# Hybrid Hyena/attention/pooling backbone: the norms' subtraction, the pooling's ends and a few priorities put elsewhere

## The chip, the cores and the metric

The kernel runs on one core of a Trainium2 chip. The metric is the device time of one execution in microseconds (us), the median of three runs. A core has TensorE (PE, matmuls; PEld is its weight load), VectorE (DVE), ScalarE (ACT), GpSimd (POOL) and SyncE (SP, which here issues most DMAs). Each engine runs its own instructions in order; semaphores order them between engines.

## The reference

Two layers over 256 latent and 256 context tokens, 1024 wide, all float32. Each layer modulates its input with a scale and a shift, makes one large input projection, and from its columns three mixers: a Hyena long convolution (a 3-tap short convolution, then a product in the frequency domain), grouped-query attention with normed queries and keys and rotary positions, and centred pooling over windows of 2, 4, 8 and 16 tokens. Each mixer has a projection and a gate; their sum goes through an output projection, a residual and a norm. A SwiGLU FFN with a residual and a norm follows. What is touched here, cut short:

```python
def layer_norm(x, g, b):
    mu = jnp.mean(xf, axis=-1, keepdims=True)
    var = jnp.mean(jnp.square(xf - mu), axis=-1, keepdims=True)
    return (xf - mu) * lax.rsqrt(var + EPS) * g + b

# pool_mixer, per group of 256 channels with window w
    lo, hi = jnp.clip(t - w // 2, 0, L), jnp.clip(t + w - w // 2, 0, L)
    mean = (csg[:, hi] - csg[:, lo]) / (hi - lo)       # fewer tokens at both ends
    outs.append(mean - uf)

# hyena_mixer: s = b + sum over 3 taps of up[:, j:j+L] * w[j]; then v, x0, x1 = split(s)

# trunk_layer
    xl = layer_norm(DN_ALPHA * xl + g1_l * stream_mixer(...), ln1_g, ln1_b)
    xl = layer_norm(DN_ALPHA * xl + g2_l * swiglu(xl * (1 + sc2_l) + sh2_l), ln2_g, ln2_b)
```

In the second layer only the latent stream is carried through (256 tokens); the context gives keys and values alone.

## The kernel before

Features lie on the 128 partitions, tokens along the free axis: a stream of activations is eight tiles of 128 features by 512 tokens in layer 0 (latent, then context) and by 256 in layer 1. A float32 product is made of three matmuls on parts: a value is split into a rounded part (hi) and the rest (lo), and hi x hi, hi x lo and lo x hi are added up in PSUM (`mm3`, L165). Weights come as 336 blocks of 128 x 1024 in the order of use (`wfetch`, L203): a DMA, ACT writes hi (L162), VectorE, or for every sixth or third block GpSimd, writes lo by a subtraction (L159). Three blocks of each are buffered. Dense products have three PSUM buffers (`mm`), other products five (`aux`).

The code is a trace of instructions. A planner at build time turns it into a fixed list per engine: whatever is ready and comes first in the trace goes first, and `high_priority(n)` counts an instruction as traced n places earlier. Side chains are Python generators in a list `bg`; each dense block calls `pump` (L130), which moves every generator in `bg` one yield further. `drain` (L150) runs all of them to their end.

A layer runs: Hyena's 24 blocks, where each of the three parts per channel block goes through `short_conv` (L535: one ACT operation, two VectorE taps, L541 and L543, which read PSUM and free it); pooling's eight blocks (`pool_in`, L574: GpSimd clears the padding, ACT copies, VectorE adds shifted copies (L593), GpSimd multiplies the first and last eight tokens (L598), VectorE finishes (L600)); keys and values (`kv`, L656, starts the generator `keys`, L689); a drain; merge of Hyena with its gate; queries; merge of pooling; attention; merge of attention; output projection; norm; FFN; norm.

A norm has two parts. While the eight tiles come out of TensorE, `ln_tile_` (L833) adds the residual (L836), ACT squares (L842), and VectorE adds up the values and squares (L846, L847). Then `ln_finish_` (L867): TensorE sums over partitions and broadcasts (`lnbc`, L852, L874); ACT squares the mean (L876), VectorE makes the variance (L877) and its root by eight steps (`newton`, L286); ACT copies the mean (L879). For each pair of tiles VectorE subtracts the mean (L884) and scales (L885), and the outputs are written, as hi and lo or as they are. In layer 0 both norms run once for each stream. In layer 1 the first norm has work beside it: TensorE takes the unnormed values through five FFN blocks, which `from_raw` (L926) corrects afterwards. The last norm is followed only by the output's DMAs.

The keys' generator, in full order of its pieces:

```python
    def keys(self, kf, sqs, kh):
        ...            # sums of squares (PE), root on 8 columns (DVE)
        yield
        ...            # krb: root spread to all partitions (PE), kf scaled (DVE), swap by DMA (POOL)
        yield
        self.rotate(kf[:, :, 0:SEQ], sw, NKV)
        self.split(kh[0], kh[1], kf)
```

`kv` calls `self.start(self.keys(...))`, which runs it to the first yield, and then, for each of two pairs of value tiles, the value matmuls, a split and `self.pump()`.

## Time and profile before

| | |
|---|---|
| three runs, median (us) | 1705.91 (1705.83 to 1708.21) |
| profiled execution, own time (us) | 1707.7 |
| its span, first to last instruction (us) | 1705.9 |
| mean granted TensorE clock, share of full | 0.989 |
| busy: TensorE, VectorE, ACT, GpSimd (us) | 1652.4, 1222.7, 708.6, 221.5 |

Busy time counts an instruction from its start to its end, and an instruction that is held up after its start is busy for that time too. A wait in the profile has the engine that waited, the line of the waiting instruction and that of the one that released it. Matmuls overlap and their ends are modelled. A granted clock of 1.00 is 2.4 GHz, one of 0.50 is 1.2 GHz; a mean between them is a share of the time at each.

### The profile page before, as it was taken

What the parts mean: (1) busy time and instruction counts of PE and PEld (TensorE: products, weight loads), DVE (VectorE), ACT (ScalarE), POOL (GpSimd) and SP (SyncE); (2) the same over time, 40 slices, a digit from 0 to 9 for tenths busy, and PEclk for the clock granted to TensorE, in tenths of its full rate; (3) what the DMA queues carried; (4) which work ended last, traced back from release to release, by engine and by line L of the source; (5) the groups of instructions that cost most, each with busy time, mean ns of one, the idle gap of its engine ahead of it and who ended that gap; (6) DMA issues with size and microseconds to landing.
All of it is one profiled execution on the core that took longest, in us unless ns stands there. A gap on an engine that the chain in (4) does not pass through costs nothing.

```text
span 1705.9 us, 25592 instructions
## 1 busy us (share of the span) xinstructions
PE 1652.4 (97%) x9926; PEld 1445.9 (85%) x9926; DVE 1222.7 (72%) x2124; ACT 708.6 (42%) x1130; POOL 221.5 (13%) x232
## 2 busy tenths in 40 slices
PE   7999999999999999999999999998899999989996
PEld 1888888788888888988888888898799999989996
DVE  4788878755677775879876577498866786796655
ACT  2534332533454432542232223274435564564442
POOL 1133542000200000000000012124510210000000
PEclk9999999999999999999999999999999999999998
DMA  8422222453422343236666654154336535645552
GB/s 315 158 87 87 74 80 76 148 161 126 136 79 93 122 156 125 92 88 197 190 200 191 211 190 149 62 165 132 100 120 191 166 100 162 195 139 185 185 185 88
DMA packets 68897, 243.34 MB, mean 143 GB/s; under 512 B 8166, under 2 KB 8744, under 8 KB 68520
## 3 DMA queue, kind: packets, MB, share of 16 engines
q1 hardware_dynamic: 67192, 236.78, 43.5%
q0 software_dynamic: 1168, 4.72, 0.9%
q8 instruction: 78, 1.28, 0.3%
q14 instruction: 43, 0.35, 0.1%
q10 hardware_dynamic: 416, 0.21, 0.1%
HBM read 238.01 MB, written 1.05 MB: 140 GB/s over the span
## 4 chain that ended last, share of the span: by engine, by line
PE 82%; DVE 12%; ACT 3%; issue 2%; POOL 1%; DMA 1%; ACTq 0%; DVEq 0%; POOLq 0%
PE f L171 6%; PE f L169 6%; PE f L170 6%; PE b L169 4%; PE g L169 4%; PE g L171 4%; PE g L170 4%; PE b L171 4%; PE b L170 4%; PE w L169 4%; PE w L170 4%; PE w L171 4%; DVE wlo L159 2%; PE ux L169 2%; PE ux L171 2%
## 5 line engine op out<-in xcount | busy, mean ns | idle before, releaser
L162 ACT ACTIVATE whi<-raw 128x1024 fp32r<-128x1024 f32 x322 | 340.7, 1059 | 700.4 <-PE f L170 153.5
L159 DVE TENSOR_TENSOR wlo<-raw,whi 128x1024 fp32r<-128x1024 f32 x311 | 399.9, 1287 | 202.2 <-ACT whi L162 199.6
L190 DVE SCALAR_TENSOR_TENSOR junk<-ada,silu 128x1024 bf16<-128x1024 f32 x128 | 158.9, 1243 | 55.6 <-DMA ada<-adat 55.0
L169 PE MATMUL f<-h2h,whi 128*128 128x512 f32 (+1 forms) x320 | 125.1, 391 | 0.1
L171 PE MATMUL f<-h2h,wlo 128*128 128x512 f32 (+1 forms) x320 | 124.6, 389 | 0.0
L170 PE MATMUL f<-h2l,whi 128*128 128x512 f32 (+1 forms) x320 | 124.6, 389 | 0.0
L169 PE MATMUL f<-h,whi 128*128 128x256 f32 x312 | 88.4, 283 | 1.9 <-DVE fraw L931 1.9
L169 PE MATMUL w<-a,whi 128*128 128x256 f32 (+1 forms) x284 | 90.2, 317 | 0.0
L170 PE MATMUL w<-a,whi 128*128 128x256 f32 (+1 forms) x284 | 89.3, 315 | 0.0
L171 PE MATMUL w<-a,wlo 128*128 128x256 f32 (+1 forms) x284 | 89.3, 314 | 0.0
L171 PE MATMUL f<-h,wlo 128*128 128x256 f32 x312 | 88.5, 283 | 0.6 <-DVE wlo L159 0.6
L170 PE MATMUL f<-h,whi 128*128 128x256 f32 x312 | 87.5, 280 | 0.0
L169 PE MATMUL g<-hh,whi 128*128 128x512 f32 x192 | 75.6, 394 | 0.0
L171 PE MATMUL g<-hh,wlo 128*128 128x512 f32 x192 | 75.4, 393 | 0.0
L170 PE MATMUL g<-hl,whi 128*128 128x512 f32 x192 | 75.3, 392 | 0.0
L169 PEld LDWEIGHTS f<-h2h,whi 128*128 128x128 f32 x320 | 60.0, 188 | 14.0 <-DVE sg L974 0.9
L171 PEld LDWEIGHTS f<-h2h,wlo 128*128 128x128 f32 x320 | 60.1, 188 | 13.6
L170 PEld LDWEIGHTS f<-h2l,whi 128*128 128x128 f32 x320 | 60.2, 188 | 13.1
L169 PEld LDWEIGHTS f<-h,whi 128*128 128x128 f32 x312 | 58.6, 188 | 2.3 <-issue 2.3
L170 PEld LDWEIGHTS f<-h,whi 128*128 128x128 f32 x312 | 59.3, 190 | 0.0
L171 PEld LDWEIGHTS f<-h,wlo 128*128 128x128 f32 x312 | 58.4, 187 | 0.8 <-DVE wlo L159 0.8
L170 PEld LDWEIGHTS w<-a,whi 128*128 128x128 f32 x284 | 53.5, 188 | 3.9 <-issue 0.2
(474 smaller groups left out, 4799.6 us busy)
## 6 DMA issues: line engine op xcount, KB each, us to landing
raw<-wst SPq DMA_DIRECT2D x336, 512.0 KB, 3.6
ada<-adat SPq DMA_DIRECT2D x80, 512.0 KB, 4.1
adar<-ada SPq DMA_DIRECT2D x16, 512.0 KB, 10.2
qsw<-q POOLq DMA_DIRECT2D x16, 128.0 KB, 5.0
x<-x_t POOLq DMA_DIRECT2D x1, 2048.0 KB, 9.7
x<-x_t SPq DMA_DIRECT2D x1, 1024.0 KB, 10.5
x<-x_t SPq DMA_DIRECT2D x2, 512.0 KB, 10.2
silu<-c_row SPq DMA_DIRECT2D x2, 512.0 KB, 8.4
```

The costliest lines, as they stand in the source:

```text
L159: (eng or self.nc.vector).tensor_tensor(out=lo, in0=src, in1=hi.bitcast(F32), op=ALU.subtract)
L162: self.nc.scalar.activation(hi, src, AF.Copy)
L169: t.matmul(out, lhsT=ah, rhs=bh, start=start, stop=False)
L170: t.matmul(out, lhsT=ah, rhs=bl, start=False, stop=False)
L171: t.matmul(out, lhsT=al, rhs=bh, start=False, stop=stop)
L190: nc.vector.scalar_tensor_tensor(out=junk, in0=raw, scalar=1.0, in1=self.silu[:, s], op0=ALU.mult, op1=ALU.mult, accum_out=mod[:, s, m : m ...
```

## The change

The subtraction of the mean (L884) becomes a function `center`. With `beside`, which is set for every norm but the second stream of layer 0's second norm, GpSimd runs all of it, issued behind ACT's copy of the mean and ahead of the root; that copy now stands ahead of the variance. Without it, VectorE subtracts as before, one pair at a time. In layer 1's first norm the additions of values and squares move to GpSimd too. The finish of the first norms has priority 100 instead of none. In layer 1 `short_conv` has priority 100. In pooling, the two memsets become one and the two products at the ends become one, both strided and on VectorE. `drain` takes a generator to leave alone, and `layer` gives it the keys' at the first drain.

```diff
--- before.py
+++ after.py
@@ -147,12 +147,13 @@
         self.bg.append(g)
         self.step(g)
 
-    def drain(self):
-        while self.bg or self.feed:
-            if not self.bg:
+    def drain(self, keep=None):
+        while self.feed or any(g is not keep for g in self.bg):
+            if all(g is keep for g in self.bg):
                 self.start(self.feed.popleft())
             for g in list(self.bg):
-                self.step(g)
+                if g is not keep:
+                    self.step(g)
 
 
     def lo_of(self, lo, src, hi, eng=None):
@@ -532,7 +533,13 @@
             hi, lo = hy[2 * qd + ci]
             self.split(hi[:, t0 : t0 + SEQ], lo[:, t0 : t0 + SEQ], y[:, ci])
 
-    def short_conv(self, l, u, ch, out, ns):
+    def short_conv(self, l, *a):
+        if l == 0:
+            return self.short_conv_(l, *a)
+        with self.tc.high_priority(100):
+            self.short_conv_(l, *a)
+
+    def short_conv_(self, l, u, ch, out, ns):
 
         nc = self.nc
         v = lambda t: t.rearrange("p (s t) -> p s t", s=ns)
@@ -581,8 +588,8 @@
             w = WINDOWS[g]
             u_ps = self.dense(h, T, "up")
             u = self.t4(shape=[P, ns, W], name="pu")
-            nc.gpsimd.memset(u[:, :, 0:PAD], 0.0)
-            nc.gpsimd.memset(u[:, :, PAD + SEQ :], 0.0)
+            eights = lambda t: t.rearrange("p s (k e) -> p s k e", e=8)
+            nc.vector.memset(eights(u)[:, :, 0 :: W // 8 - 1], 0.0)
             nc.scalar.activation(u[:, :, PAD : PAD + SEQ], u_ps.rearrange("p (s t) -> p s t", s=ns), AF.Copy)
 
             cur, step, lo, hi = u, 1, 0, W
@@ -594,9 +601,9 @@
                                         in1=cur[:, :, nlo + b : nhi + b], op=ALU.add)
                 cur, lo, hi = nx, nlo, nhi
                 step *= 2
-            for e, ec in ((PAD, 0), (PAD + SEQ - 8, 8)):
-                nc.gpsimd.tensor_tensor(out=cur[:, :, e : e + 8], in0=cur[:, :, e : e + 8],
-                                        in1=self.edge[:, g : g + 1, ec : ec + 8].to_broadcast([P, ns, 8]), op=ALU.mult)
+            ends = eights(cur[:, :, PAD : PAD + SEQ])[:, :, 0 :: SEQ // 8 - 1]
+            nc.vector.tensor_tensor(out=ends, in0=ends, in1=self.edge[:, g : g + 1].rearrange("p o (a e) -> p o a e", e=8).to_broadcast([P, ns, 2, 8]),
+                                    op=ALU.mult)
             nc.vector.scalar_tensor_tensor(out=po[:, c].rearrange("p (s t) -> p s t", s=ns), in0=cur[:, :, PAD : PAD + SEQ],
                                            scalar=1.0 / w, in1=u[:, :, PAD : PAD + SEQ], op0=ALU.mult, op1=ALU.subtract)
 
@@ -669,7 +676,8 @@
             nc.scalar.activation(kf[:, hh], o, AF.Copy, scale=self.v(l, V_KG))
             sqs.append(sq)
             self.pump()
-        self.start(self.keys(kf, sqs, kh))
+        self.kgen = self.keys(kf, sqs, kh)
+        self.start(self.kgen)
         wa, wb = self.wblock(1), self.wblock(0)
         for tp in range(2):
             o = self.mm([P, 2, 256], name="v")
@@ -816,9 +824,9 @@
                 nc.vector.scalar_tensor_tensor(out=x, in0=x, scalar=scale, in1=cb, op0=ALU.mult, op1=ALU.subtract)
             yield
 
-    def ln_start(self, y, s, g, pt, pf):
+    def ln_start(self, y, s, g, pt, pf, beside=True, sums=None):
         ts = slice(s * SEQ, (s + 1) * SEQ)
-        st = dict(y=y[:, :, ts], g=g[:, s], s=s, pt=pt, pf=pf)
+        st = dict(y=y[:, :, ts], g=g[:, s], s=s, pt=pt, pf=pf, beside=beside, sums=sums or self.nc.vector)
         st["acc"] = self.t2b(shape=[P, 2, SEQ], name="lnacc")
         return st
 
@@ -843,8 +851,8 @@
         if m == KT - 1:
             st["sq"] = sq
             return
-        nc.vector.tensor_tensor(out=acc[:, 0], in0=y[:, 0] if m == 1 else acc[:, 0], in1=d, op=ALU.add)
-        nc.vector.tensor_tensor(out=acc[:, 1], in0=acc[:, 1], in1=sq, op=ALU.add)
+        st["sums"].tensor_tensor(out=acc[:, 0], in0=y[:, 0] if m == 1 else acc[:, 0], in1=d, op=ALU.add)
+        st["sums"].tensor_tensor(out=acc[:, 1], in0=acc[:, 1], in1=sq, op=ALU.add)
 
     def ln_sums(self, st):
 
@@ -874,14 +882,24 @@
             nc.tensor.matmul(bc[:, i], lhsT=self.ones, rhs=src, start=False, stop=i == 1)
         rm = st["rm"] = self.t2b(shape=[P, 2, SEQ], name="lnrm")
         nc.scalar.activation(t, bc[:, 0], AF.Square)
+        nc.scalar.activation(rm[:, 1], bc[:, 0], AF.Copy)
+        steps = [((0, 1), (1, 1)), ((2, 2),), ((4, 2),), ((6, 2),)]
+
+        def center(e, i):
+            for m, n in steps[i // 2]:
+                e.tensor_tensor(out=y[:, m : m + n], in0=y[:, m : m + n], in1=rm[:, 1:2].to_broadcast([P, n, SEQ]), op=ALU.subtract)
+
+        if st["beside"]:
+            for i in range(0, KT, 2):
+                center(nc.gpsimd, i)
         nc.vector.scalar_tensor_tensor(out=a, in0=bc[:, 1], scalar=EPS, in1=t, op0=ALU.add, op1=ALU.subtract)
         self.newton(rm[:, 0], a, t)
-        nc.scalar.activation(rm[:, 1], bc[:, 0], AF.Copy)
         yield
         for i in range(0, KT, 2):
-            for m, n in ((i, 1), (i + 1, 1)) if i == 0 else ((i, 2),):
+            if not st["beside"]:
+                center(nc.vector, i)
+            for m, n in steps[i // 2]:
                 yn = y[:, m : m + n]
-                nc.vector.tensor_tensor(out=yn, in0=yn, in1=rm[:, 1:2].to_broadcast([P, n, SEQ]), op=ALU.subtract)
                 nc.vector.scalar_tensor_tensor(out=yn, in0=yn, scalar=1.0 / RS, in1=rm[:, 0:1].to_broadcast([P, n, SEQ]), op0=ALU.mult, op1=ALU.mult)
             for kind, dst, a, b, *at in outs:
                 td = slice(at[0], at[0] + SEQ) if at else ts
@@ -1027,7 +1045,7 @@
         self.pool_in(l, h, T, po)
         self.lo_pool = 0
         kh, vh = self.kv(l, [(h, 0, 512)] if hc is None else [(h, 0, SEQ), (hc, SEQ, SEQ)])
-        self.drain()
+        self.drain(self.kgen)
         if not last:
             self.bg.append(self.filter_hidden(l + 1))
         mg = self.big(F32, [P, KT, T], name="mg")
@@ -1057,7 +1075,7 @@
         al = self.scaled(self.v(l, V_LN1G, 8), self.v(l, V_LN1B, 8))
         fo = [self.fold(self.v(l, V_LN1G, 8), self.v(l, V_LN1B, 8), mod[4][:, s], mod[3][:, s]) for s in range(ns)]
         raw = self.raw_pair(*fo[0]) if ns == 1 else None
-        lns = [self.ln_start(y, s, mod[2], (20, 50)[l], 0) for s in range(ns)]
+        lns = [self.ln_start(y, s, mod[2], (20, 50)[l], 100, sums=(None, nc.gpsimd)[l]) for s in range(ns)]
         if raw:
             lns[0]["raw"] = raw, fo[0][0]
         for m in range(KT - nb):
@@ -1094,7 +1112,7 @@
         g, b = self.v(l, V_LN2G, 8), self.v(l, V_LN2B, 8)
 
         def start():
-            return [self.ln_start(y, s, mod[5], 0, (100, 0)[l]) for s in range(ns)]
+            return [self.ln_start(y, s, mod[5], 0, (100, 0)[l], s == 0) for s in range(ns)]
 
         if last:
             def finish(s, st):
```

## Rows read from the trace of the kernel before

**Rows 1.** Page, part 1: engine, busy us, share of the span, instructions.
```profile
PE 1652.4 (97%) x9926; PEld 1445.9 (85%) x9926; DVE 1222.7 (72%) x2124; ACT 708.6 (42%) x1130; POOL 221.5 (13%) x232
```

**Rows 2.** Waits of TensorE, whole span: line <- releaser: total us, times, longest.
```profile
PE up L171 <- DVE wlo L159: 8.4, 1, 8.4
...
PE ux L169 <- DVE zx L543: 5.0, 1, 5.0
...
PE krb L323 <- DVE diag L322: 2.4, 1, 2.4
PE f L273 <- ACT h2h L891: 2.1, 1, 2.1
...
PE u L273 <- ACT h L891: 1.7, 1, 1.7
PE lnbc L852 <- DVE lnacc L847: 1.7, 1, 1.7
```

**Rows 3.** By stretch: length, then PE, PEld, DVE, ACT, POOL busy; clock, DMA.
```profile
1112.00:1160.00 48.00, 45.90 (x356) 44.84 (x356) 47.40 (x84) 36.23 (x60) 10.82 (x7) 0.96 0.53 168
1160.00:1205.00 45.00, 40.49 (x307) 39.77 (x308) 35.86 (x57) 18.58 (x28) 22.11 (x15) 0.92 0.43 129
1205.00:1241.00 36.00, 27.61 (x213) 27.21 (x211) 33.02 (x42) 11.46 (x19) 20.41 (x39) 0.86 0.32 103
```

**Rows 4.** Timeline, last norm: start, us, engine, line, operation, shapes, idle before.
```profile
1692.07 0.38 ACT L876 ACTIVATE lnacc<-lnbc 128x256 f32<-128x256 f32 x1 [0.79 <-PE lnbc L874]
...
1692.95 0.29 DVE L290 TENSOR_SCALAR lnrm<-lnacc 128x256 int32<-128x256 int32 x1
...
1693.62 0.42 DVE L884 TENSOR_TENSOR x<-x,lnrm 128x256 f32<-128x256 f32 x1
1693.95 0.42 DVE L298 TENSOR_TENSOR lnacc<-lnacc 128x256 f32<-128x256 f32 x1
...
1694.96 0.68 DVE L884 TENSOR_TENSOR x<-x,lnrm 128x512 f32<-128x512 f32 x1
1695.56 0.42 DVE L301 SCALAR_TENSOR_TENSOR lnrm<-lnacc,lnrm 128x256 f32<-128x256 f32 x1
...
1698.35 0.42 DVE L885 SCALAR_TENSOR_TENSOR x<-x,lnrm 128x256 f32<-128x256 f32 x1
```

**Rows 5.** Timeline, GpSimd: two operations of two SBUF inputs.
```profile
465.03 1.29 POOL L631 TENSOR_TENSOR mg<-mg,sg 128x512 f32<-128x512 f32 x1 [12.60 <-DVE sg L629]
...
1153.88 0.74 POOL L566 TENSOR_TENSOR zx<-vv,x 128x256 f32<-128x256 f32 x1 [6.73 <-DVE x L543]
```

**Rows 6.** Timeline, VectorE and GpSimd: instructions that overlap.
```profile
465.17 2.23 DVE L159 TENSOR_TENSOR wlo<-raw,whi 128x1024 fp32r<-128x1024 f32 x1 [0.22 <-ACT whi L162]
...
1125.28 2.40 POOL L159 TENSOR_TENSOR wlo<-raw,whi 128x1024 fp32r<-128x1024 f32 x1 [1.25 <-ACT whi L162]
...
1126.15 1.69 DVE L290 TENSOR_SCALAR lnrm<-lnacc 128x256 int32<-128x256 int32 x1
```

**Rows 7.** Timeline, VectorE: weight splits inside the roots of layer 0's norms.
```profile
734.14 1.23 DVE L159 TENSOR_TENSOR wlo<-raw,whi 128x1024 fp32r<-128x1024 f32 x1
...
1109.69 1.22 DVE L159 TENSOR_TENSOR wlo<-raw,whi 128x1024 fp32r<-128x1024 f32 x1
```

**Rows 8.** Timeline, VectorE: the two taps at the 5.0 us wait.
```profile
1156.82 0.47 DVE L541 SCALAR_TENSOR_TENSOR zx<-ux,vecs,zx 128x255 f32<-128x255 f32 x1
...
1162.63 0.47 DVE L543 SCALAR_TENSOR_TENSOR zx<-ux,vecs,zx 128x255 f32<-128x255 f32 x1
```

**Rows 9.** Timeline, VectorE and GpSimd: pooling's ends handed over.
```profile
272.64 0.69 DVE L600 SCALAR_TENSOR_TENSOR po<-pb,pu 128x512 f32<-128x512 f32 x1 [2.79 <-POOL pb L598]
...
1228.33 0.36 POOL L598 TENSOR_TENSOR pb<-pb,edge 128x8 f32<-128x8 f32 x2
...
1228.72 1.47 DVE L600 SCALAR_TENSOR_TENSOR x<-pb,pu 128x256 f32<-128x256 f32 x1 [1.09 <-POOL pb L598]
```

**Rows 10.** Timeline, TensorE: the keys' broadcast between value matmuls.
```profile
289.14 0.42 PE L170 MATMUL v<-wlo,hh 128*128 128x256 f32 x1
289.36 1.06 PE L323 MATMUL krb<-diag,ones 128*128 128x128 f32 x4
290.07 0.56 PE L171 MATMUL v<-whi,hl 128*128 128x256 f32 x1
```

## The prediction, made before the changed kernel was run

> **What bounds the kernel now.** I read the page's busy shares first. TensorE is busy 97% of the span [rows 1], so an edit elsewhere pays only where it shortens a stall of TensorE or the tail, when TensorE has nothing left. Then the waits of TensorE by name [rows 2]: the reader is to see that nearly all ends on VectorE, in four kinds of place. In layer 1's Hyena and pooling stages a dense block waits 5.0 us for VectorE's short convolution (L543 frees the PSUM buffer) and another 8.4 us for a weight split. In layer 0's key stage there are 2.4 us. Around the norms there are 2.1 us (first norm, layer 0), 1.7 us (second norm, layer 0) and 1.7 us (first norm of layer 1, waiting for the sums, L847). And the last norm is a tail with no matmul behind it. Last, the table by stage [rows 3]: VectorE is busy 47.40 of 48 us at layer 1's start, 35.86 of the next 45 and 33.02 of the last 36, and the granted clock of TensorE, on a mean of its two levels of 2.4 and 1.2 GHz, falls from 0.96 to 0.92 and 0.86 where the stalls are. VectorE in that stage is as near to a bound as TensorE.
>
> The sum below is a difference. The profiled execution took 1707.7 us (span 1705.9, 1.8 around it); the three timed runs have the median 1705.91, so I add the difference to that median. About 0.2%, 3.4 us, is what can be told from no change.
>
> **Subtraction of the mean on GpSimd.** In the tail VectorE runs the eight steps of the root and the five subtractions (L884) interleaved, from 1692.95 to the first scaling (L885) at 1698.35, 5.4 us with no hole [rows 4]. From start to next start a subtraction of 256 columns holds it 0.33 us and one of 512 columns 0.60, so the five cost 2 x 0.33 + 3 x 0.60 = 2.5 us. GpSimd does an operation of two SBUF inputs in 0.74 us at 256 columns and 1.29 at 512 [rows 5]: 2 x 0.74 + 3 x 1.29 = 5.35 us. Were the two engines independent, VectorE would gain at most 2.5 us less the wait for ACT's copy of the mean, now ahead of the root (0.35), and less some 0.6 for dependent steps that nothing fills: 1.5 us earlier. But they are not. A weight split of 1.22 us takes 2.23 when it starts 0.14 us after a GpSimd operation of 1.29, and ends one own length after it; the root's first step (L290) takes 1.69 instead of 0.29 while GpSimd has a 2.40 us split [rows 4, 6]. One waits for the other's whole instruction. The root's steps depend on each other, so between any two GpSimd gets in. Tail, step by step: GpSimd starts at 1692.8 (the square on ACT from 1692.07 to 1692.45, 0.38 [rows 4], and a copy of the same size behind it); five subtractions 5.35 with L290 (0.25) and four steps (0.35 each) taking turns with them, 7.0; three more steps at 0.43, 1.3; first scaling at 1701.1 instead of 1698.35. **Tail: +2.7 us, bounds -1.5 and +2.9.**
> The row of L290 shows the blocking for one step of the root only. The Trainium skill, page "SBUF — State Buffer", section "Who interferes with whom", says that a VectorE instruction with two SBUF inputs and a GpSimd instruction that reads SBUF exclude each other, the second to issue blocking fully; that covers every later step of the root too, it speaks against this change, and by it the tail is the +2.7 above, while with L290 alone blocked it would be about -1.
>
> Second norm of layer 0, first stream: the same exchange, 5.35 - 2.5 = +2.9, but two weight splits now lie inside the root (the later one in [rows 7], 1.14 us from its start to the next). If one goes out, +1.7. TensorE waits for this norm already (u, 1.7 us, [rows 2]), so all of it lands on the path. **+1.7, bounds -1.7 (its stall gone) and +3.2.**
>
> First norm of layer 0, two streams: GpSimd adds 2 x 5.35 = 10.7 and VectorE loses 2 x 2.5 = 5.0. Priority 100 pushes up to two splits behind (2.3; one of them in [rows 7]) and five adds from PSUM (L836, 0.4 each) can lie beside GpSimd, having one SBUF input. Net +5.7 at most, +1.4 at least; VectorE is without a hole up to the second stream's first scaling, and TensorE waits 2.1 us there [rows 2]. I take the value nearer the low end, since the priority is written in the edit: **+2.5, bounds -3.8 (stall and a like clock loss gone) and +5.7.**
>
> First norm of layer 1: the sums move as well, 12 additions of 256 columns at 0.34 (4.1 us) become 12 of 0.74 (8.9 us); the splits to and beside them go on. The last sum is late today: TensorE waits for it (lnbc, [rows 2]). Net +4.8, or +2.5 if six PSUM adds lie beside: +3.6. The subtraction costs 2.9 more, against which two splits leave the root's steps (2.3): +0.6. Queued behind the late sum on TensorE are the norm's own broadcast and the five raw FFN blocks. **+4.2, bounds -2.5 and +7.** The four places: **+11.1 us.**
>
> **Short convolution first, layer 1.** At the 5.0 us stall the first tap (L541) ran at 1156.82 and the second (L543) at 1162.63 [rows 8]; between them seven instructions of the Hyena units and a norm. At priority 100 the second follows at about 1157.3, so the PSUM buffer is free 5 us earlier. But the next block needs a weight split, and that stands behind the same seven instructions in a stage where VectorE is full [rows 3]. What can be won is VectorE's idle time afterwards, 45 - 35.86 = 9.1 us, of which most is waiting for a TensorE that is itself at work: I take a third. **-3.0, bounds -8.6 (5.0, and all the clock lost in the stage, 0.08 x 45) and +1 (splits pushed behind).**
>
> **Pooling's ends on VectorE.** Removed from GpSimd: per block two memsets and two products (0.36 a pair, [rows 9]). Added to VectorE: one memset and one product, not in the trace; between 0.15 (a step on 8 columns) and 0.36 each, so 2.4 to 5.8 us for 8 blocks; I take 0.2, the arithmetic being tiny, 3.2 us. Gone is the hand-over: L600 waited 2.79 us with VectorE idle in layer 0, and 1.09 plus a blocked 1.0 in layer 1, as GpSimd had other work ahead [rows 9]. Layer 1: idle 36 - 33.02 = 3.0 won, GpSimd's 2.9 out of the way, 3.2 added, some of the rest filled: **-2.0, bounds -13.4 (stall 8.4 and 0.14 x 36 of clock) and +2.** Layer 0: 2.79 won less half of the added work, just ahead of the 2.4 us stall of the keys: **-2.0, bounds -4.8 (the stall and as much clock) and +1.** Sum of both parts with the convolution: **-7.0.**
>
> **Keys.** The edit keeps the keys' generator out of the drain. It has two yields: its first piece runs when it is started, the second at the pump after the first pair of value tiles, the third at the pump after the second. It is finished before the drain is called; the trace has its broadcast between value matmuls [rows 10]. Cost and gain 0.
>
> **How the numbers follow.** +11.1 - 7.0 = +4.1, 1705.9 + 4.1 = **1710.0 us**, by a lock that no hand-over between the two engines avoids.
>
> Rivals. (1) The stalls of layers 1 and 0 go nearly in full: short convolution -6, pooling -9 and -4, norms as priced: -8, about **1698**. For it: [rows 2] names exactly these waits. Against: VectorE's 47.40 of 48 us [rows 3], it can't run ahead. (2) GpSimd really works beside: tail -1.5, the two norms of layer 0 -1.7 and -3.8, layer 1's -2.5, others -7: **1690**. Against it stand [rows 6]. The skill's page "Perfetto Trace Analysis", section "Optimizing Scalar/DVE Operations", grants that moving work off a saturated VectorE may make sense, then warns of the shared read port; by its first half this rival would hold, and the traces so far bear out the second. (3) Slower still: each engine runs a list fixed ahead; if the list was made as though the subtractions cost VectorE nothing, TensorE's matmuls on norm outputs stand too early in its queue and later independent blocks can't pass them. It decides once the norm is late by more than the 2 us of today's stalls, and costs about another 2 us at four places: **1718**. (4) The parts cancel, or the keys' edit does move the chain and takes its 2.4 us stall away: **1705.5**.
>
> Chances: forecast 0.42 (1706 to 1715; of this 0.30 slower, 0.12 within), rival 1 0.27 (0.25 faster, 0.02 within), rival 2 0.08 (faster), rival 3 0.13 (slower), rival 4 0.10 (within). That is faster 0.33, within 0.2% 0.24, slower 0.43. The range 1694 to 1719 leaves out rival 2 and the far ends of rivals 1 and 3. The forecast's own range is 1706 to 1715.
>
> **What would show it.** In the tail: root steps stretched from 0.42 to about 1.0 to 1.7 us, with GpSimd's subtractions between, and L885 some 2.7 us later after the last broadcast. In layer 1's first norm: the wait of lnbc for the sums above 1.7 us. L541 and L543 next to each other in layer 1, and the 5.0 us wait gone but a wait for a split in its place. No wait of L600 for GpSimd. The keys' matmuls still between the value matmuls. I am wrong if the root's steps keep 0.42 us under GpSimd, or if the up and ux waits disappear with nothing in their place.

## The result, and the profile after

| | before | after |
|---|---|---|
| median (us) | 1705.87 (1705.18 to 1708.21) | 1723.6 (1722.15 to 1724.41) |
| ratio | | 1.0100, interval 1.0087 to 1.0114 |
| span of the profiled execution (us) | 1705.9 | 1721.7 |
| mean granted clock | 0.989 | 0.985 |

The change makes the kernel 17.7 us slower (medians of four runs each); 4.1 had been forecast, and the result lies above the range. The busy times answer to [rows 1]:

```profile
PE 1660.5 (96%) x9926; PEld 1452.2 (84%) x9926; DVE 1235.2 (72%) x2119; ACT 707.8 (41%) x1130; POOL 258.8 (15%) x205
```

VectorE runs five instructions less and is busy 12.5 us longer than before. TensorE's waits answer to [rows 2] (line <- releaser: total us, times, longest):

```profile
PE f L170 <- DVE x L844: 5.7, 1, 5.7
PE u L274 <- ACT h L909: 4.1, 2, 2.6
PE lnbc L860 <- POOL lnacc L855: 4.0, 1, 4.0
PE uv L172 <- DVE wlo L160: 3.4, 1, 3.4
PE hfrow L435 <- DVE pu L592: 2.5, 1, 2.5
...
PE k L170 <- ACT pu L593: 1.8, 1, 1.8
...
PE k L172 <- POOL wlo L160: 1.7, 1, 1.7
```

The waits of 8.4 us (up), 5.0 (ux) and 2.4 (krb) are gone. In their place stand waits at the norms (the first three rows) and smaller ones, of which the split's 3.4 is the longest. The stages of [rows 3], with bounds moved to the same TensorE instructions (length; PE, PEld, DVE, ACT, POOL busy; clock, DMA):

```profile
1117.30:1167.80 50.50, 48.06 (x357) 46.02 (x357) 45.76 (x83) 33.99 (x56) 13.12 (x6) 0.93 0.48 155
1167.80:1215.40 47.60, 40.90 (x309) 39.72 (x308) 39.48 (x60) 21.47 (x33) 22.93 (x15) 0.93 0.40 128
1215.40:1246.70 31.30, 26.90 (x213) 25.88 (x212) 30.92 (x41) 11.02 (x19) 18.46 (x11) 0.98 0.31 101
```

The last stage, layer 1's pooling up to its first key block, is 4.7 us shorter and its granted clock is 0.98 instead of 0.86; the two before it are 2.5 and 2.6 us longer. At layer 1's first norm the granted clock goes the other way. The same 280 TensorE instructions, before, in the run `subtract` (explained below) and in the changed kernel:

```profile
1490.00:1530.00 40.00, 35.65 (x280) 33.89 (x279) 37.26 (x81) 28.15 (x54) 0.00 (x0) 1.00 0.44 135
...
1492.40:1537.60 45.20, 39.56 (x280) 37.23 (x279) 39.73 (x78) 28.66 (x55) 6.63 (x5) 0.89 0.40 125
...
1496.50:1544.40 47.90, 39.53 (x279) 37.15 (x279) 40.14 (x75) 28.66 (x55) 9.97 (x9) 0.89 0.38 118
```

A mean of 0.89 over 47.9 us is as much as 0.11 x 47.9 = 5.3 us of full clock not granted; some of it falls into waits, so it is at most that much of the 8 us lost at this place. Over the whole span, 1721.7 x 0.015 less 1705.9 x 0.011 gives some 7 us of the 15.8 by which the span is longer. Following one and the same TensorE instruction through both traces, the difference of its start grows or shrinks at these places (us):

| place | forecast | changed kernel | parts alone |
|---|---|---|---|
| pooling and keys, layer 0 | -2.0 | +0.8 | pool +0.7, ends -1.7, padding +0.6 |
| first norm, layer 0 | +2.5 | +4.3 | subtract +1.9, first +2.1 |
| second norm, layer 0 | +1.7 | +3.5 | subtract +3.3 |
| Hyena, layer 1 | -3.0 | +2.5 | conv +1.5 |
| pooling and keys, layer 1 | -2.0 | -3.8 | pool -3.7, ends -0.9, padding -2.2 |
| first norm, layer 1 | +4.2 | +8.0 | subtract +5.2, first +4.7, sums +1.9 |
| tail | +2.7 | +1.5 | subtract +1.5, tail +1.5 |

Each entry is from one profiled execution. Runs whose code is unchanged at a place differ by up to 1.5 us there (tail and ends at layer 0's first norm, subtract at the keys of layer 0), so a single entry of that size proves nothing. Where the second norm of layer 0 ends and the Hyena stage begins is loose too; the sum of the two, +6.0, is firmer than either. At layer 0's first norm that is the granted clock: 0.96 over 45 us before, 1.00 in tail. Timed alone, the five parts add up to 11.1 + 8.4 + 2.4 + 0.3 - 5.3 = 16.9, against 1.0% of 1705.9 = 17.1 for the whole. That the two agree is in part luck, since two of the parts hide each other (nopriority and vsubtract, below).

### The profile page after: what moved, and what is told of

It reads as the page before. It is cut to its first block, busy times and chain, and to the rows that moved or that the text cites. A ratio compares the mean times of both kernels' runs of the same rounds, so it can differ in the third digit from the quotient of the medians.

```text
span 1721.7 us, 25557 instructions
## 1 busy us (share of the span) xinstructions
PE 1660.5 (96%) x9926; PEld 1452.2 (84%) x9926; DVE 1235.2 (72%) x2119; ACT 707.8 (41%) x1130; POOL 258.8 (15%) x205
## 4 chain that ended last, share of the span: by engine, by line
PE 83%; DVE 10%; ACT 2%; issue 2%; DMA 1%; POOL 1%; ACTq 0%; DVEq 0%; POOLq 0%
PE f L170 7%; PE f L172 7%; PE f L171 7%; PE b L170 4%; PE g L170 4%; PE g L172 4%; PE g L171 4%; PE b L172 4%; PE b L171 4%; PE w L170 3%; PE w L172 3%; PE w L171 3%; PE ux L170 2%; PE ux L172 2%; PE ux L171 2%
## 5 line engine op out<-in xcount | busy, mean ns | idle before, releaser
L890 POOL TENSOR_TENSOR x<-x,lnrm 128x512 f32<-128x512 f32 (+1 forms) x25 | 29.7, 1219 | 353.5 <-ACT lnrm L885 353.5
```

The lines of the kernel that those rows point to most:

```text
L890: e.tensor_tensor(out=y[:, m : m + n], in0=y[:, m : m + n], in1=rm[:, 1:2].to_broadcast([P, n, SEQ]), op=ALU.subtract)
```

## Experiments

Each kernel is the one before with one edit, unless it says otherwise. Ratios are to the kernel before on the same chip, with 95% intervals.

**turns**: seven short series behind the last norm; only VectorE's step and GpSimd's operation differ.

```diff
+                if n and g == "one":
+                    nc.gpsimd.tensor_copy(z, k)
+                elif n and g == "set":
+                    nc.gpsimd.memset(z, 1.0)
+                else:
+                    nc.gpsimd.tensor_tensor(out=b, in0=b, in1=a, op=ALU.add)
...
+                if g == "psum":
+                    nc.vector.tensor_tensor(out=v, in0=pz[:, 0:SEQ], in1=v, op=ALU.add)
...
+                else:
+                    nc.vector.tensor_tensor(out=v, in0=v, in1=c, op=ALU.add)
```

> The kernel before with seven short series behind its last norm, each on its own: ten VectorE steps of 256 columns, the first six of them as long as GpSimd's own series of five 512-column operations lasts beside them. Series 1: GpSimd idle. 2: GpSimd adds two SBUF inputs. 3: GpSimd copies one SBUF input. 4: GpSimd only writes (memset). 5: as 2, but VectorE's step has one input in PSUM. 6: as 2, but VectorE's step has a single SBUF input. 7: as 2, but VectorE's steps don't depend on each other. Theory A (whole instructions take turns whenever both engines read SBUF through what they share): series 1 and 4 0.42 to 0.46 us a step, series 2 and 7 1.3 to 1.8 us for the steps beside GpSimd, series 5 0.42 to 0.5; 6 slow too, as L290's 1.69 us in the trace of before suggests. Theory C (GpSimd slows VectorE by a share of bandwidth): 0.5 to 0.8 in series 2, 3, 6 and 7 alike. Theory D (only dependent steps are held, independent ones keep the port): series 7 at 0.42 while GpSimd waits.

Timeline, VectorE's ten steps and GpSimd's five operations of each series (start, us in total, line):

```profile
1708.11 4.56 DVE L1225 TENSOR_TENSOR vv<-vv,out 128x256 f32<-128x256 f32 x10
...
1713.63 9.67 DVE L1225 TENSOR_TENSOR vv<-vv,out 128x256 f32<-128x256 f32 x10
1714.25 6.93 POOL L1213 TENSOR_TENSOR zz<-zz,silu 128x512 f32<-128x512 f32 x5
...
1724.32 6.40 DVE L1225 TENSOR_TENSOR vv<-vv,out 128x256 f32<-128x256 f32 x10
1724.93 3.68 POOL L1209 COPY zz<-silu 128x512 f32<-128x512 f32 x5
...
1731.74 4.96 DVE L1225 TENSOR_TENSOR vv<-vv,out 128x256 f32<-128x256 f32 x10
1732.35 2.85 POOL L1211 MEMSET zz<- 128x512 f32 x5
...
1737.73 4.55 DVE L1219 TENSOR_TENSOR vv<-pz,vv 128x256 f32<-128x256 f32 x10
1738.35 6.62 POOL L1213 TENSOR_TENSOR zz<-zz,silu 128x512 f32<-128x512 f32 x5
...
1745.93 8.71 DVE L1221 TENSOR_SCALAR vv<-vv 128x256 f32<-128x256 f32 x10
...
1755.54 9.30 DVE L1223 TENSOR_TENSOR vv<-ss,out 128x256 f32<-128x256 f32 x10
```

Ten steps alone take 4.56 us. Beside five additions on GpSimd they take 9.67, dependent, and 9.30, independent: about 1.0 us more for each GpSimd operation, and theories C and D fall. In every series with GpSimd the first step still meets an addition; where VectorE reads SBUF alone that costs it 0.4 to 0.5, which is all that the memsets' series loses. A copy costs 0.29 (five steps of 0.71 instead of 0.42), a memset nothing, and with one input in PSUM nothing is lost (4.55). So the hold is on VectorE steps that read only SBUF beside GpSimd operations that read it. By the Trainium skill, page "SBUF — State Buffer", section "Who interferes with whom", a VectorE instruction with two SBUF inputs contends with a GpSimd instruction that reads SBUF and not with one that only writes; the series agree (1.37 us a step beside additions and 0.71 beside copies, 0.42 beside memsets).

**tail** and **subtract**: `center` on GpSimd in the last norm alone, and at all places of the change. Where GpSimd subtracts, ACT's copy of the mean stands ahead of the variance too, as in the change.

```diff
+        if st["beside"]:
+            for i in range(0, KT, 2):
+                center(nc.gpsimd, i)
...
+                if not st["beside"]:
+                    nc.vector.tensor_tensor(out=yn, in0=yn, in1=rm[:, 1:2].to_broadcast([P, n, SEQ]), op=ALU.subtract)
```

> The kernel before with the subtraction on GpSimd in the last norm alone; everything before that norm is unchanged, so all of the difference lies behind the last broadcast. Theory A (taking turns): the first scaling some 1.9 us later behind that broadcast than before, the kernel +1.5 to +2.7. Rival C (two independent engines): -1.5, steps of 0.42. The profiled span is to move by what the tail moves by, within 1 us.

> The kernel before with the subtraction of the mean on GpSimd at the four places of the change, and nothing else of it: sums on VectorE, the first norms' finish without priority, convolution and pooling as before. Theory A (VectorE and GpSimd take turns whole instruction by whole instruction): about +9 us, of which the tail +1.5 to +2.7, second norm of layer 0 +3.5, first norm of layer 0 +2, first norm of layer 1 +2; the root's last steps 1.0 to 1.4 us instead of 0.42 wherever GpSimd subtracts. Rival B (the subtraction is the whole of the change's loss at the norms): about +17. Rival C (GpSimd works beside VectorE, what is lost at the norms comes from priority and sums): between -5 and +1.

Measured: tail 1.0009 (0.9999 to 1.002), +1.5 us behind the last broadcast in its trace, with the first scaling 1.9 us later as expected; the span, which was to move as much, did not (1705.8), since places with unchanged code were shorter by as much (layer 0's first norm by 1.5, at a clock of 1.00 for 0.96). subtract 1.0065 (1.0045 to 1.0085), +11.1 us. Theory A holds against C. Its +9 was too little, most of all at layer 1's first norm (+5.2 for +2), and a rival that it didn't name is the granted clock there, 0.89 for 1.00 (above): it is 0.66 from 1497.5 to 1502.5 us, a fall that begins right behind TensorE's wait of 1.7 us for the sums, which before has too, and 4 us ahead of the first subtraction. So part of the +5.2 isn't the subtraction's. The timeline of subtract there:

```profile
1501.76 6.63 POOL L883 TENSOR_TENSOR x<-x,lnrm 128x256 f32<-128x256 f32 x5 [74.27 <-ACT lnrm L878]
...
1502.66 1.69 DVE L159 TENSOR_TENSOR wlo<-raw,whi 128x1024 fp32r<-128x1024 f32 x1
1504.28 1.52 DVE L297 TENSOR_TENSOR lnacc<-lnrm 128x256 f32<-128x256 f32 x1
1505.83 1.41 DVE L298 TENSOR_TENSOR lnacc<-lnacc 128x256 f32<-128x256 f32 x1
...
1508.60 1.22 DVE L159 TENSOR_TENSOR wlo<-raw,whi 128x1024 fp32r<-128x1024 f32 x1
```

Two weight splits are still inside the root, and the steps beside GpSimd take 1.4 to 1.5 us. From the variance to the first scaling it is 9.9 us, 1.5 more than before. The rest of the 5.2 is the clock and TensorE's later wait for the first correction (`fraw`, 3.2 us instead of 1.9). At layer 0's second norm subtract has

```profile
1108.84 1.21 DVE L159 TENSOR_TENSOR wlo<-raw,whi 128x1024 fp32r<-128x1024 f32 x1
```

as the only split in the root, where before has two, at 1108.22 and 1109.69 [rows 7].

**first**: priority 100 for the first norms' finish, nothing else.

```diff
-        lns = [self.ln_start(y, s, mod[2], (20, 50)[l], 0) for s in range(ns)]
+        lns = [self.ln_start(y, s, mod[2], (20, 50)[l], 100) for s in range(ns)]
```

> The kernel before with priority 100 for the finish of the first norms alone; the subtraction stays on VectorE. Theory P (with this priority the first stream's finish stands in VectorE's list ahead of the second stream's residual adds, and TensorE waits for the PSUM buffers that these free): +2 to +4 in layer 0, with a wait of f for x (the residual add) of 2 us or more that before doesn't have; 0 in layer 1, where there is one stream. Rival Q (the order costs only once GpSimd stretches the finish, so it takes both): 0 within 1. Rival R (the weight splits go behind and the norm comes earlier, as the edit means it): -1 to -2.5.

Measured: 1.0049 (1.0033 to 1.0065), +8.4 us, without moving any work to GpSimd. Its waits of TensorE that before doesn't have:

```profile
PE wo L169 <- DVE x L836: 3.5, 1, 3.5
...
PE lnc L804 <- ACT x L910: 2.2, 1, 2.2
PE f L169 <- DVE sg L974: 2.1, 1, 2.1
```

The first is theory P in layer 0: the first stream's finish stands ahead of the second stream's residual adds, which free the PSUM buffers. The other two are in layer 1, where theory P expected nothing. Four runs followed them.

**equal**: first, with the tiles' priority 100 higher in both layers and, in layer 1, `from_raw` at 100. **root** and **rest**: the priority for the finish up to the root, or behind it, and 1 for the other pieces. **one**: 1 instead of 100. The edits are those of equal, root (rest has `"rm" in st`) and one.

```diff
+        lns = [self.ln_start(y, s, mod[2], (120, 150)[l], 100) for s in range(ns)]
...
+                with self.tc.high_priority(100):
+                    return self.from_raw(o, lns[0]["rm"])
```

```diff
+            first = st["pf"] == 100 or "rm" not in st
+            with self.tc.high_priority(st["pf"] if first else 1):
```

```diff
+        lns = [self.ln_start(y, s, mod[2], (20, 50)[l], 1) for s in range(ns)]
```

> The kernel 'first' (finish of the first norms at priority 100) with what it passes raised by as much: the residual adds and sums of the tiles in both layers (120 and 150 instead of 20 and 50), and in layer 1 the corrections of the five raw FFN blocks (100). Theory P (the loss of 'first' is that the finish passes residual adds in layer 0 and raw corrections in layer 1): layer 0's first norm within 1 us of before (2.1 later in 'first'), layer 1's within 2 (4.7 later in 'first'), the whole 0 to +3. Rival W (the loss is that the finish passes weight splits): as much loss as in 'first' or more, +6 to +10.

> The kernel before with the first norms' finish at priority 100 (101) in its first piece alone, up to the root. Theory E (the pieces behind the root do the harm, by filling ACT and VectorE with outputs that TensorE doesn't wait for yet, and in layer 0 by passing the second stream's residual adds): layer 1's first norm within 1 us of before, layer 0's within 1, the kernel within 2 of before. Rival F (the root's piece does it, by passing weight splits): +4 to +8, most of what 'first' loses.

> The kernel before with that priority in the pieces behind the root alone. Theory E: +5 to +9, as 'first', with waits of TensorE for residual adds in layer 0 (about 3.5) and for the copies of x and for sg in layer 1 (about 2 each). Rival F: 0 to +2.

> The kernel before with the first norms' finish at priority 1 in place of none (100 in the change). Theory G (any priority at all makes the planner order the finish by kinds, all scalings, then all eight hi's, then the lo's; in layer 1 TensorE waits for the first corrections and copies behind them): layer 1's first norm +4.5 to +7 as in 'first', layer 0's within 1.5 of before or less, the kernel +3 to +6. Rival H (it needs the 100 places): both norms within 1.5 of before, the kernel within 2.

| | ratio | first norm, layer 0 | first norm, layer 1 |
|---|---|---|---|
| first | 1.0049 (1.0033 to 1.0065) | +2.1 | +4.7 |
| equal | 1.0012 (0.9999 to 1.0024) | -3.7 | +7.4 |
| root | 1.0002 (0.9988 to 1.0016) | -3.7 | +6.9 |
| rest | 1.0015 (1.0003 to 1.0027) | -0.6 | +5.4 |
| one | 1.0017 (1.0007 to 1.0028) | +0.2 | +3.1 |

In layer 0 the loss is gone once the adds aren't passed (equal): theory P holds there. The priority is then even a gain, -3.7, of which 0.04 x 45 = 1.8 is the granted clock (1.00 in equal, 0.96 before). In layer 1 theory P, theory E and rival F all fail, since every variant loses; and since the 1 that root and rest set for the other pieces loses by itself (one), these two don't tell which piece does it. What they share shows in ACT's timeline, here of one:

```profile
1505.23 4.17 ACT L891 ACTIVATE h<-x,fold 128x256 fp32r<-128x256 f32 x8 [6.30 <-DVE x L885]
1509.30 1.57 ACT L894 ACTIVATE lnt<-x,fold 128x256 f32<-128x256 f32 x3
```

and of the kernel before:

```profile
1506.39 1.10 ACT L891 ACTIVATE h<-x,fold 128x256 fp32r<-128x256 f32 x2 [5.83 <-DVE x L885]
1507.40 0.58 ACT L894 ACTIVATE lnt<-x,fold 128x256 f32<-128x256 f32 x1
1507.89 1.08 ACT L891 ACTIVATE h<-x,fold 128x256 fp32r<-128x256 f32 x2
```

With any priority, even 1, the planner's list has the finish by kinds, eight hi's in a row; without one it goes pair by pair. The lo's and the copies of x come later, and TensorE waits for the copies (lnc: 3.6 us in one). That fits theory G's mechanism; its sizes were too high (+3.1 at the norm for +4.5 to +7, +2.9 in all for +3 to +6). Why the planner orders so stays open. The loss varies with the granted clock over this norm: 0.92 in first, rest and one, 0.89 in equal and root, 1.00 before. That tells how far the loss is clock, not what makes the clock fall in one and not in another.

**sums**: the additions of layer 1's first norm on GpSimd.

```diff
-        nc.vector.tensor_tensor(out=acc[:, 0], in0=y[:, 0] if m == 1 else acc[:, 0], in1=d, op=ALU.add)
+        st["sums"].tensor_tensor(out=acc[:, 0], in0=y[:, 0] if m == 1 else acc[:, 0], in1=d, op=ALU.add)
```

> The kernel before with the additions of values and squares of layer 1's first norm on GpSimd alone. Theory A (GpSimd 0.74 us for an addition instead of 0.34, taking turns with VectorE, and the last sum is what TensorE waits for): +2 to +4, lnbc waiting for the sums 3 to 5 us instead of 1.7. Rival C (VectorE is freed of 4.1 us and the rest of the stage gains it): -1 to -2. Rival S (the sums matter only beside the subtraction): 0 within 1.

Measured: 1.0014 (1.0003 to 1.0024), +2.4 us, and lnbc waits 4.0 us for L847 on GpSimd. Theory A. Here too the granted clock is lower at this norm, 0.96 for 1.00.

**conv**: `short_conv` of layer 1 at priority 100.

```diff
+        with self.tc.high_priority(100):
+            self.short_conv_(l, *a)
```

> The kernel before with the short convolution of layer 1 at priority 100 alone. The prediction on record: -3. Theory A (VectorE has no slack in this stage, the weight splits go back by as much as the taps come forward): +1 to +3, with the 5.0 us wait for the second tap gone and a wait for a weight split of 2 to 4 us in its place. Rival C (the stall goes and nothing takes its place): -4 to -6.

Measured: 1.0002 (0.9989 to 1.0014). Waits of TensorE in its Hyena stage:

```profile
PE ux L171 <- DVE wlo L159: 3.0, 2, 2.7
...
PE ux L169 <- DVE x L549: 2.1, 1, 2.1
...
PE uv L171 <- DVE wlo L159: 1.5, 1, 1.5
...
PE uv L169 <- DVE vv L549: 1.1, 1, 1.1
```

The 5.0 us wait is gone, and waits of 3.0 + 2.1 + 1.5 + 1.1 = 7.7 stand where 5.0 + 1.3 + 0.3 = 6.6 had been. Nothing that can be measured is won or lost alone: rival C is out, and so is the forecast of -3.0; theory A's waits came, its +1 to +3 is not shown.

**pool**, **padding**, **ends**: both edits of pooling, the memset alone (the first piece below), the products alone (the second).

```diff
-            nc.gpsimd.memset(u[:, :, 0:PAD], 0.0)
-            nc.gpsimd.memset(u[:, :, PAD + SEQ :], 0.0)
+            nc.vector.memset(eights(u)[:, :, 0 :: W // 8 - 1], 0.0)
...
-                nc.gpsimd.tensor_tensor(out=cur[:, :, e : e + 8], in0=cur[:, :, e : e + 8],
...
+            nc.vector.tensor_tensor(out=ends, in0=ends, in1=self.edge[:, g : g + 1].rearrange("p o (a e) -> p o a e", e=8).to_broadcast([P, ns, 2, 8]),
```

> The kernel before with pooling's padding and ends on VectorE alone, both layers. The prediction on record: -4 (-2 in each layer). Theory A (the memset on VectorE stands in line until its tile buffer comes free, which costs layer 0 some 3 us at the last blocks of pooling; the ends themselves gain): layer 0 +1 with a wait of hfrow for the memset of about 2.5 us, layer 1 -4, together -3. Rival C (memset and ends both only gain): -6 to -9. Rival D (the gain of layer 1 in the changed kernel came from the convolution in front of it, not from pooling): 0 to +3.

> The kernel before with pooling's padding cleared by one memset on VectorE, the ends left on GpSimd. Theory A (the memset stands in line on VectorE until the tile's buffer comes free, holding up what is queued behind it): layer 0 +2.5 to +3 at pooling with hfrow waiting for that memset, of which the keys give back what their 2.4 us wait was; layer 1 between -1 and +2, so 0 to +3 in all. Rival D (the memset on VectorE is what gained in layer 1, by taking the clearing off GpSimd): -4 to -6.

> The kernel before with the products at pooling's ends on VectorE, the padding left on GpSimd. Theory A (the hand-over to GpSimd and back is what cost, and only this part of the edit gains): -5 to -8, the wait of up for the weight split (8.4) mostly gone, no wait of hfrow for a memset, and the wait of krb (2.4) kept or shorter. Rival D (padding is what gained): 0 to -1.5 and the 8.4 us wait still there.

Measured: pool 0.9969 (0.9957 to 0.9981), -5.3 us; padding 1.0004 (0.9994 to 1.0015); ends 0.9984 (0.9972 to 0.9997), -2.7. Both together gain, as forecast. Alone, the products gain 2.7 (-5 to -8 had been expected) and leave 6.9 us of the 8.4 us wait of up, nearer to rival D; the memset takes that wait to 2.0 but gains nothing that can be measured (rival D: -4 to -6). Why both together gain more than the two alone stays open. Theory A's account of layer 0, a memset that stands in line for its buffer, is wrong. The timeline of padding at the wait for it:

```profile
217.89 3.90 POOL L517 TENSOR_TENSOR zf<-dfts 128x512 f32<-128x512 f32 x2 [7.67 <-DVE dfts L514]
...
218.36 2.31 DVE L159 TENSOR_TENSOR wlo<-raw,whi 128x1024 fp32r<-128x1024 f32 x1
...
220.59 1.28 DVE L433 TENSOR_SCALAR diag<-ident,hfrs 128x128 f32<-128x128 f32 x1
...
221.93 0.38 PE L434 MATMUL hfrow<-diag,ones 128*1 128x128 f32 x2 [2.39 <-DVE pu L585]
```

and of before:

```profile
217.12 1.22 DVE L159 TENSOR_TENSOR wlo<-raw,whi 128x1024 fp32r<-128x1024 f32 x1
217.29 4.04 POOL L517 TENSOR_TENSOR zf<-dfts 128x512 f32<-128x512 f32 x2 [7.55 <-DVE dfts L514]
```

The memset takes 0.09 us and waits for nothing; the profile names it because it came last. What TensorE needs is diag, and diag is late because the weight split now starts behind GpSimd's L517 instead of ahead of it and takes 2.31 us for 1.22: turns again.

**nopriority** and **vsubtract**: the changed kernel without the finish's priority, and with the subtraction on VectorE.

```diff
-        lns = [self.ln_start(y, s, mod[2], (20, 50)[l], 100, sums=(None, nc.gpsimd)[l]) for s in range(ns)]
+        lns = [self.ln_start(y, s, mod[2], (20, 50)[l], 0, sums=(None, nc.gpsimd)[l]) for s in range(ns)]
```

```diff
-        lns = [self.ln_start(y, s, mod[2], (20, 50)[l], 100, sums=(None, nc.gpsimd)[l]) for s in range(ns)]
+        lns = [self.ln_start(y, s, mod[2], (20, 50)[l], 100, beside=False, sums=(None, nc.gpsimd)[l]) for s in range(ns)]
...
-            return [self.ln_start(y, s, mod[5], 0, (100, 0)[l], s == 0) for s in range(ns)]
+            return [self.ln_start(y, s, mod[5], 0, (100, 0)[l], False) for s in range(ns)]
```

> The changed kernel with the finish of the first norms back at no priority; all else of the change stays. Theory of separate prices (priority and taking turns each cost their own): -8 against the changed kernel, so +9 to +10 against before; layer 0's first norm +2 instead of +4.3, layer 1's first norm +5 to +7 instead of +8. Rival O (once GpSimd subtracts, the priority costs little, since the finish waits for GpSimd anyway): within 3 of the changed kernel, +14 to +18 against before.

> The changed kernel with the subtraction of the mean back on VectorE at all places, behind ACT's early copy as in the change; priority, sums, convolution and pooling as in the change. Theory of separate prices: -11 against the changed kernel, so +6 to +7 against before; the tail as before within 0.5, layer 1's first norm +5 to +7. Rival O: the priority alone makes layer 1's loss, so that norm stays at +8 and the kernel is at +9 to +12.

Measured: nopriority 1.009 (1.0075 to 1.0106), vsubtract 1.0052 (1.0037 to 1.0067). Of the subtraction's 11.1 us, 17.1 - 8.9 = 8.2 come back, of the priority's 8.4 only 17.1 - 15.4 = 1.7. In layer 0's first norm the prices are separate: nopriority loses 1.7 there instead of 4.3. In layer 1's first norm they aren't: 7.2 us without the priority, 7.0 without the subtraction, 8.0 with both. There each hides most of the other. For nopriority rival O is right (+14 to +18); vsubtract's +8.9 and 7.0 lie between it and the separate prices.

**nosplit**, **nosum**, **vector**: pool, and then GpSimd's weight splits, Hyena's frequency sums of layer 1 (L514, L517), and the rest of its arithmetic on VectorE, one on top of the other.

```diff
-        self.lo_pool = (0, 6)[l]
-        self.lo_pool = 3
...
-            nc.gpsimd.tensor_tensor(out=zf[:, par], in0=y[:, :, 0], in1=y[:, :, 1], op=op)
+            (nc.gpsimd if l == 0 else nc.vector).tensor_tensor(out=zf[:, par], in0=y[:, :, 0], in1=y[:, :, 1], op=op)
```

> The kernel 'pool' with all weight splits on VectorE: none goes to GpSimd in pooling and layer 1's Hyena. Theory A (a split of 2.4 us on GpSimd holds VectorE up for about as long as VectorE's own split of 1.22 takes, or longer): -5 to -8 against before, and the 3.4 us splits of VectorE gone. Rival L (VectorE, busy 47 of 48 us in layer 1's first stage, has no room for ten more splits): -2 to +5.

> The kernel 'nosplit' with Hyena's frequency sums of layer 1 (L514, L517, 1.3 us each on GpSimd) on VectorE too. Theory A: a further 0 to -4, since 16 x 1.3 us of GpSimd that exclude VectorE become 16 x 0.6 on it. Rival L (no room on VectorE): +2 to +8 against 'nosplit', with longer waits of TensorE for weight splits in layer 1's Hyena stage.

> The kernel 'nosum' with the rest of GpSimd's arithmetic on VectorE too: Hyena's products (L566) and sums of layer 0, the second merge (L631), the keys' and queries' rotation, the filters' sums. Theory of turns: 0 to -4 against 'nosum' (another 100 us of GpSimd that exclude VectorE become 50 on it, but where neither bounds), -24 to -27 against before. Rival L (VectorE has no room left or dependent chains get longer): +2 to +10 against 'nosum'.

Measured: nosplit 0.9924 (0.9908 to 0.9939), -13 us; nosum 0.9871 (0.9853 to 0.9889), -22; vector 0.9869 (0.9851 to 0.9887), no more than nosum and where -24 to -27 had been expected. Rival L is out in all three. Theory A has the direction, but its sizes missed: nosplit and nosum gained more than it gave them (-5 to -8, and 0 to -4 on top). The splits on VectorE in pool, then in nosplit (count, busy us, mean ns):

```profile
L159 DVE TENSOR_TENSOR wlo<-raw,whi 128x1024 fp32r<-128x1024 f32 x311 | 400.7, 1290 | 207.9 <-ACT whi L162 205.9
```

```profile
L159 DVE TENSOR_TENSOR wlo<-raw,whi 128x1024 fp32r<-128x1024 f32 x321 | 411.4, 1283 | 212.1 <-ACT whi L162 210.1
```

Page of nosum:

```profile
PE 1644.0 (98%) x9926; PEld 1438.6 (86%) x9926; DVE 1219.0 (73%) x2182; ACT 708.6 (42%) x1130; POOL 163.9 (10%) x142
```

VectorE takes ten splits more for 10.7 us, yet its whole busy time falls from 1228.4 in pool to 1224.0 in nosplit, and in nosum it is below that of before [rows 1]. The 47.40 us for 84 instructions [rows 3] are 44.89 for 88 in nosum over the same TensorE instructions: part of what looked like a full engine was time held up. How much of the gain is the hold and how much that VectorE has a split done in 1.2 us where GpSimd took 2.5, these runs don't separate. Some 12 of nosum's 24.7 us of span are granted clock (0.996 for 0.989).

The **keys'** edit was not run alone. By the code, the generator has ended before the drain is called, and the changed kernel has the keys' broadcast (`krb`) between value matmuls, as before [rows 10].

## Why the prediction was right and wrong

**Direction, and the mechanism at the tail: right.** The tail does what was worked out:

```profile
1707.21 5.65 POOL L890 TENSOR_TENSOR x<-x,lnrm 128x256 f32<-128x256 f32 x5 [192.38 <-ACT lnrm L885]
1707.62 0.46 DVE L291 TENSOR_SCALAR lnrm<-lnacc 128x256 int32<-128x256 int32 x1
1708.11 0.83 DVE L298 TENSOR_TENSOR lnacc<-lnrm 128x256 f32<-128x256 f32 x1
1708.97 1.37 DVE L299 TENSOR_TENSOR lnacc<-lnacc 128x256 f32<-128x256 f32 x1
1710.37 1.37 DVE L301 SCALAR_TENSOR_TENSOR lnacc<-lnacc 128x256 f32<-128x256 f32 x1
...
1713.17 0.42 DVE L298 TENSOR_TENSOR lnacc<-lnrm 128x256 f32<-128x256 f32 x1
```

The steps that were 0.42 us [rows 4] take 1.37 beside GpSimd. The size was off: a step and a subtraction together take 1.40 us from start to start, where the sum took 1.29 + 0.35 = 1.64. From GpSimd's start to the first scaling it is 7.4 us (1714.62 less 1707.21), not 8.3. Behind the last broadcast the first scaling comes 1.9 us later and the end 1.5, not 2.7.

**What the result exceeds the forecast by.** Alone, against the forecast's terms: the subtraction +11.1 for +7.5 (2.7 + 1.7 + 2.5 + 0.6), the priority +8.4 for nothing of its own, the sums +2.4 for +3.6, the convolution +0.3 for -3.0, pooling -5.3 for -4.0. So the steps that failed are the priority, taken for a help; the convolution's gain; and a term that has no entry at the norms, the granted clock, which the forecast counted only as something to be won back. Inside the whole the priority's share is smaller (1.7 us come back without it).

**Second norm of layer 0.** +3.3 alone, not +1.7. The credit for a split was had: one of the two left the root, and the first scaling comes only 1.0 us later behind its broadcast. The rest comes behind it: TensorE waits for the hi's (h) a second time, 3.7 us in all instead of 1.7, and its granted clock is 0.50 from 1112 to 1116 and 0.64 to 1120 (0.73 and 0.85 before). The bound of +3.2 was the better value by luck.

**First norm of layer 0.** The subtraction's +1.9 lies inside the forecast, and so does the changed kernel's +4.3. The step that failed is the priority: it was entered as a help (splits pushed behind), and what it pushed behind was the second stream's residual adds, for which TensorE waits 5.7 us in the changed kernel. Who is queued behind a raised instruction was asked for splits only. With the adds raised as well (equal) the help is there.

**First norm of layer 1.** The sums' wait came as said (lnbc 4.0 us); they were put at +3.6 and cost 1.9 here. The subtraction was put at +0.6, on a credit of 2.3 for two splits leaving the root, and its run lost 5.2: the splits stayed, the root took 1.5 us longer, and the rest is TensorE's later wait and the granted clock. Setting a priority costs 4.7 alone, with the order that the planner then makes; the forecast had nothing for it. The three don't add up: the place lost 8.0, at a clock of 0.89.

**Short convolution.** -3.0 forecast, nothing alone, +2.5 inside the change. A third of VectorE's 9.1 us of idle time was taken as gain. The weight split that takes the wait's place was named; its price was not entered in full. There was room all the same: nosum has the second stage of [rows 3] in 40.6 us instead of 45, by taking work off GpSimd and not by an order.

**Pooling.** Layer 1 gained 3.8 (forecast 2.0) and gives back part of its 8.4 us at the keys, in the two waits of k. Layer 0 was forecast at -2.0 and shows +0.8: the changed order puts a split into GpSimd's turn. The products alone show -1.7 there, about as much as runs with unchanged code differ by.

**Rivals.** 1 and 2 are out, 2 by the series of turns. Rival 3 (1718) came nearest; its mechanism, matmuls that stand too early in TensorE's list, was not tested, and the excess that was found lies in the priority, the convolution, one credit for splits and the clock, so its nearness is luck as far as is known. Rival 4 is out.

**What would show it.** Seen: the stretched steps, lnbc's wait, the 5.0 us wait turned into waits for splits, no wait of pooling for GpSimd's ends, the keys between the value matmuls. Not as said: the first scaling 2.7 us later (1.9).

## What to carry to other kernels

Price an operation that reads SBUF on GpSimd as time taken from VectorE (here 1.0 us for 512 columns, against 0.60 if VectorE does it itself), and don't count a busy share of 15% as free room. A priority has to be priced by everything that it passes on each engine's list, and by the order inside what it raises. Measure the parts of a change alone: one of these five gained 5.3 us and was buried under the others. Read the granted clock at every place that gains or loses: here at most 5.3 of the 8.0 us lost at one norm, and some 12 of the 24.7 that nosum won.

## What was not expected of the hardware

A GpSimd copy with a single input holds VectorE too (0.29 us each in turns), and a VectorE step with a single SBUF input, 0.29 us alone (the last steps of its series), is held like one with two: 8.71 us for ten beside five additions. A step with an input in PSUM isn't held at all. And moving work to the slower engine raised the faster one's busy time. The page of subtract:

```profile
PE 1657.2 (97%) x9926; PEld 1448.8 (84%) x9926; DVE 1229.6 (72%) x2099; ACT 707.2 (41%) x1130; POOL 254.8 (15%) x257
```

VectorE has 25 instructions fewer than before [rows 1] and is busy 6.9 us more; in nosum it has 58 more and is busy 3.7 less.
